# Two chunks of the hidden columns replaced by two passes over the rows, with the intermediate y kept in DRAM

## The chip, the cores and the metric

The kernel runs on one core of one Trainium2 chip. Its engines work at the same time, each through its own list of instructions: PE (TensorE) multiplies, DVE (VectorE) and ACT (ScalarE) add, scale and move results, POOL (GpSimd) and SP (SyncE) are used here mainly to start DMA transfers. The metric is device time of one execution in microseconds; several executions give a median. A separate profiled execution gives the span from its first to its last instruction and all rows below.

## The reference

The program computes two matrix products with a bias and a relu between them:

```python
x: (16, 512, 768)   w1: (768, 3072)   b1: (3072,)   w2: (3072, 768)     # all fp32
y = np.maximum(np.matmul(x, w1) + b1, 0)
return np.matmul(y, w2).astype(np.float32)
```

x has 8192 rows in all. The kernel holds operands as fp16 and sums in fp32 PSUM banks.

## The kernel before

**Products by sums.** Neither product is computed block by block in the plain way. Both use a bilinear scheme of the Strassen kind: sums and differences of blocks are made ahead of the multiplication, fewer products of such sums are formed, and the outputs are sums and differences of these products. Tables give each scheme: `X_SUMS` and `W1_SUMS` list the sums of operands, `FIRST_U` and `FIRST_V` say which two operands each product takes, `FIRST_OPS` says how a finished PSUM bank is evicted ("out" to the result, "sum" into an fp32 slot s, "seed" into the bank of another chain, with a bias where the table has one), and `FIRST_ORDER` is the order of the products. `Y_SUMS`, `W2_SUMS`, `SECOND_U`, `SECOND_V` and `SECOND_OPS` do the same for the second product.

**Chunks and blocks.** The 3072 hidden columns are cut into 2 chunks of 1536, the rows into 8 blocks of 1024. There are 16 iterations, 8 blocks of the first chunk and then 8 of the second (`plan` L1457, `iteration` L1479, `iteration_end` L1497). One iteration runs the first product of its block and chunk, then the second, and y never leaves SBUF.

First product (`add_first`): x as 4 row quarters of 256 by 2 halves of K, w1 as 2 halves of K by 3 thirds of the chunk, in 2 groups of 256 columns per third. A group takes 20 products where the plain form has 24. A product is 6 matmuls 128x256 (L1101). Evictions: ACT L1137 (512 wide) and L1141 (two halves of 256 with their own bias column), DVE L1144 (a custom instruction that adds a kept sum, applies the relu and writes y), L1147 and L1152. Iteration 0 runs its first product in the plain form (`first_block`, `plain` L998, evicted by ACT L1006), because no sum exists yet.

Second product (`add_second`): y as 4 by 4 blocks, w2 as 4 by 2, 26 products where the plain form has 32. A product is 6 matmuls 128x384 (L1229) into a pair of banks; evictions on ACT L1240 and DVE L1246. Sums of y are made on DVE (L1073, 28 per iteration, 8 of them in 4 fused instructions of 1536 columns), sums of x at L841 (16 per block), of w1 at L857 (12 per group and chunk), of w2 at L875 (18 per chunk). The first chunk's outputs are stored (L1279, SP, and L1281 and L1284), those of the second chunk are added to them in DRAM by accumulating DMAs of POOL (L1281, L1284); the last iteration loads the earlier outputs instead and adds them on chip (L1289).

**Loading.** x comes in by POOL DMAs that cast to fp16 (L717) and is transposed by SP DMAs (L772). The first block is transposed on PE instead (L938, with copies on DVE L946 and ACT L944): the first 512 rows come from SP and ACT queues as fp32, the second 512 by POOL as fp16. w1 strips come by POOL (L696), w2 by POOL (L702); the second chunk's weights are cast into DRAM in time and loaded by SP at iteration 8 (L1490, L1536). DVE makes tables of bias sums at the start (L973, L977) from b1, which PE turns (L958) and DVE copies (L962). ACT squares x, w1 and w2 (L780, L889, L903), sums of which must lie in a range at the end; otherwise `general_path` computes everything again.

**What sets the order.** All work is recorded as tasks with a cost, the tiles that it reads and writes, and a due time; a planner (`Graph.run`) then writes out one fixed order for each engine. An engine does not change its order later: an instruction that waits holds all behind it on that engine.

## Time and profile before

| | |
|---|---|
| time, median of 3 runs | 846.57 us (846.46 to 846.88) |
| span of the profiled execution | 845.1 us |
| profiled span against the median | 1.5 us less |
| PE busy | 838.5 us, 99% of the span |
| DVE busy | 735.7 us, 87% |
| ACT busy | 567.3 us, 67% |
| POOL busy | 172.5 us, 20% |
| DMA traffic | 128.93 MB, mean 153 GB/s |

Busy shares are means over stages that differ. A group row of the profile gives line, engine, operation, tiles and shape, then the number of instructions, busy time and mean duration in ns, then idle time ahead of them with what ended it. Where instructions of one engine overlap, busy time over count is less than the mean duration. The chain of work is a list of pieces: start, length, what ran.

### The profile page before, as it was taken

What the parts mean: (1) busy time and instruction counts of PE and PEld (TensorE: products, weight loads), DVE (VectorE), ACT (ScalarE), POOL (GpSimd) and SP (SyncE); (2) the same over time, 40 slices, a digit from 0 to 9 for tenths busy, and PEclk for the clock granted to TensorE, in tenths of its full rate; (3) what the DMA queues carried; (4) which work ended last, traced back from release to release, by engine and by line L of the source; (5) the groups of instructions that cost most, each with busy time, mean ns of one, the idle gap of its engine ahead of it and who ended that gap; (6) DMA issues with size and microseconds to landing.
All of it is one profiled execution on the core that took longest, in us unless ns stands there. A gap on an engine that the chain in (4) does not pass through costs nothing.

```text
span 845.1 us, 16822 instructions
## 1 busy us (share of the span) xinstructions
PE 838.5 (99%) x6383; PEld 625.4 (74%) x6383; DVE 735.7 (87%) x1229; ACT 567.3 (67%) x1199; POOL 172.5 (20%) x186
## 2 busy tenths in 40 slices
PE   9999999999999999999999999999999999999997
PEld 7668778686786867768687686877868678686874
DVE  5899988969789697988999979798896979979787
ACT  4866876779677684856858568766757666456462
POOL 6210011102011010110031503324041240501303
PEclk9999999999999999999999999999999999999999
DMA  9997498978988678593893977979789797986926
GB/s 210 205 180 189 84 221 115 166 180 132 215 113 162 158 133 190 104 226 136 238 176 67 190 127 123 186 106 178 127 128 147 118 172 113 143 138 76 177 86 169
DMA packets 171127, 128.93 MB, mean 153 GB/s; under 512 B 93964, under 2 KB 169508, under 8 KB 171044
## 3 DMA queue, kind: packets, MB, share of 16 engines
q0 software_dynamic: 56592, 68.82, 53.2%
q1 hardware_dynamic: 113984, 58.02, 29.0%
q8 instruction: 50, 0.82, 0.4%
q10 hardware_dynamic: 468, 1.00, 0.3%
q14 instruction: 33, 0.27, 0.1%
HBM read 73.54 MB, written 69.21 MB: 169 GB/s over the span
## 4 chain that ended last, share of the span: by engine, by line
PE 99%; DMA 1%; ACT 0%; issue 0%; ACTq 0%
PE ps L1229 48%; PE ps L1101 47%; PE ps L998 4%; DMA s<-in_x_dram 1%; PE ps L938 1%; ACT s L1240 0%; PE ps L958 0%; PE ps L1427 0%; PE ps L1438 0%; ACTq L1240 0%
## 5 line engine op out<-in xcount | busy, mean ns | idle before, releaser
L1229 PE MATMUL ps<-v,y 128*128 128x384 f16 x2496 | 408.2, 326 | 0.0
L1101 PE MATMUL ps<-x,v 128*128 128x256 f16 x3600 | 395.6, 273 | 0.0
L1101 PEld LDWEIGHTS <-v 128*128 128x128 f16 x3600 | 352.2, 98 | 42.3
L1229 PEld LDWEIGHTS <-y 128*128 128x128 f16 x2496 | 244.2, 98 | 159.9
L1240 ACT ACTIVATE s<-ps 128x384 f32<-128x384 f32 (+1 forms) x245 | 153.1, 643 | 125.4 <-PE ps L1229 124.9
L1073 DVE TENSOR_TENSOR y<-y 128x768 f16<-128x768 f16 (+1 forms) x384 | 219.0, 617 | 2.5
L1144 DVE CUSTOM_DVE_ANT_0 y<-ps,s 128x512 f16<-128x512 f32 x240 | 155.9, 685 | 52.9 <-ACT s L1141 40.1
L1281 POOL DMA_DIRECT2D out_dram<-s x78 | 93.9, 1475 | 144.8 <-ACT s L1240 91.8
L1141 ACT ACTIVATE s<-ps,bt 128x256 f32<-128x256 f32 x180 | 75.1, 469 | 62.8 <-PE ps L1101 56.5
L841 DVE TENSOR_TENSOR x<-x 128x768 f16<-128x768 f16 (+1 forms) x210 | 113.4, 577 | 1.2
L1141 ACT ACTIVATE y<-ps,bt 128x256 f16<-128x256 f32 x180 | 69.4, 485 | 10.8 <-PE ps L1101 10.8
L1240 ACT ACTIVATE ps<-ps 128x384 f32<-128x384 f32 (+1 forms) x143 | 67.0, 507 | 6.5 <-PE ps L1229 3.2
L1246 DVE TENSOR_TENSOR s<-ps,s 128x768 f32<-128x768 f32 x74 | 70.5, 952 | 0.9
L717 POOL DMA_DIRECT2D xn<-in_x_dram x30 | 25.9, 863 | 213.3 <-DMA x<-xn 101.0
L1246 DVE TENSOR_TENSOR s<-s,ps 128x768 f32<-128x768 f32 x60 | 57.0, 950 | 2.1
L780 ACT ACTIVATE junk<-xn 128x768 f16<-128x768 f16 x64 | 53.9, 843 | 0.3
L1284 POOL DMA_DIRECT2D out_dram<-s x15 | 17.8, 1184 | 168.6 <-ACT s L1240 156.9
L1141 ACT ACTIVATE ps<-ps,bt 128x256 f32<-128x256 f32 x60 | 26.7, 445 | 32.4 <-PE ps L1101 31.4
L1137 ACT ACTIVATE ps<-ps 128x512 f32<-128x512 f32 x60 | 35.3, 588 | 4.8 <-DVE y L1144 4.0
L1152 DVE TENSOR_TENSOR s<-s,ps 128x512 f32<-128x512 f32 x30 | 20.6, 687 | 17.8 <-PE ps L1101 17.8
L998 PE MATMUL ps<-x,v 128*128 128x256 f16 (+1 forms) x216 | 31.8, 308 | 0.0
L1147 DVE SCALAR_TENSOR_TENSOR s<-ps,bt,s 128x256 f32<-128x256 f32 x60 | 26.1, 476 | 4.4 <-PE ps L1101 4.4
(61 smaller groups left out, 310.0 us busy)
## 6 DMA issues: line engine op xcount, KB each, us to landing
out_dram<-s POOLq DMA_DIRECT2D x93, 384.0 KB, 8.6
out_dram<-s SPq DMA_DIRECT2D x69, 384.0 KB, 7.0
xn<-in_x_dram POOLq DMA_DIRECT2D x28, 768.0 KB, 9.6
v<-in_w_dram POOLq DMA_DIRECT2D x16, 192.0 KB, 7.6
x<-out_dram SPq DMA_DIRECT2D x14, 192.0 KB, 2.4
w1d<-in_w_dram POOLq DMA_DIRECT2D x6, 384.0 KB, 6.6
w2d<-in_w_dram POOLq DMA_DIRECT2D x12, 192.0 KB, 5.0
v<-w1d SPq DMA_DIRECT2D x12, 192.0 KB, 4.8
```

Of the source, the lines that this page charges most:

```text
L780: self.nc.scalar.activation(out=self.junk, in_=self.xn[:, s, :], func=ACTF.Square, accum_out=self.stat[:, self.stat_at["x"] + i:][:, 0:1])
L841: self.nc.vector.tensor_tensor(out=self.two(x, out), in0=self.two(x, in0), in1=self.two(x, in1), op=ALU.add if sign > 0 else ALU.subtract)
L998: nc.tensor.matmul(self.ps[:, ps.at[0], cols], lhsT=self.v1[:, gi, 2 * h + k2, k, j * P:(j + 1) * P], rhs=rhs, start=(first and k2 == 0 an ...
L1073: self.nc.vector.tensor_tensor(out=self.two(self.y, out), in0=self.two(self.y, in0), in1=self.two(self.y, in1), op=ALU.add if sign > 0 els ...
L1101: nc.tensor.matmul(self.ps[:, at, j * self.QM:(j + 1) * self.QM], lhsT=self.v1[:, gi, self.w1s[c][gi][FIRST_V[p]], k, j * P:(j + 1) * P], ...
L1137: nc.scalar.activation(out=out, in_=ps, scale=float(a), func=func if kind == "out" else ACTF.Copy)
L1141: nc.scalar.activation(out=out[:, j], in_=ps[:, j], func=func, scale=float(a), bias=beta(j))
L1144: nc.vector._custom_dve(TENSOR_ADD_SAT, out=out, in0=ps, in1=s, s0=F_MAX, s1=0.0)
L1229: nc.tensor.matmul(self.ps[:, bank[ch].at[j], 0:NH], lhsT=self.y[:, ys[SECOND_U[p]], m0:m0 + P], rhs=self.v2[:, slot[SECOND_V[p]], h, :], ...
L1240: nc.scalar.activation(out=out, in_=ps, func=ACTF.Copy, scale=float(a))
L1246: engine.tensor_tensor(out=out, in0=in0, in1=in1, op=ALU.add if a == b else ALU.subtract)
L1281: nc.gpsimd.dma_start(out=rows, in_=out, accum_op=ALU.add)
```

## The change

The two chunks go; in their place stand two passes over all rows.

- **Pass 1** forms the first product for all 8 blocks with all 3072 columns. x stays 4 by 2 blocks, w1 becomes 2 by 4, in 3 groups of 256 columns; a group takes 26 products where the plain form has 32 (L1077, 6 matmuls 128x256 each). The 39 rows of `FIRST_OPS` per group are 20 on ACT (13 with bias, as two halves of 256 each, L1105; 7 of 512, L1100) and 19 on DVE (10 custom instructions, L1111, and 9 plain ones, L1114, all 512 wide). Groups 0 and 1 of block 0 are plain (`PLAIN = 2`, L979), so 22 group passes use the scheme. Sums: 19 of x per block (L775), 18 of w1 per group (L787). The bias tables take 13 and 6 instructions (L946, L950) in place of 8 and 4.
- **y goes to DRAM**: results are written to 9 slots `yo` and stored by SP (384 stores of 128 KB, L961).
- **w2**: POOL casts it into DRAM during pass 1 (24 DMAs, L682). In the last block SP loads it into slots of v that w1 has left (24 loads), and DVE makes 18 sums for each of 3 groups, 54 in all (L847). They then stay for the whole of pass 2.
- **Pass 2** runs 16 half blocks of 512 rows (128 of each quarter). y comes back by SP (256 loads of 192 KB, L1174), DVE makes 28 sums per half block, none fused (L1191), and a product is 6 matmuls 128x384 over K quarters of 768 (L1228). Evictions are 384 wide, ACT L1244 and DVE L1248. Outputs are stored once by SP (L1258); accumulating POOL DMAs are left for half block 0 alone (`APART = (0,)`).
- **Checks** of the range re-read x, w1 and the cast w2 in pass 2 by 56 POOL DMAs (L873), squared by ACT (L877).
- x slots, y slots and their sums share one pool z of 46 slots. `EARLY` goes from 5 to 4: the second 512 rows of x are loaded and turned after 4 strips of w1 in place of 5.

PE's instructions go from 3600 to 3432 scheme matmuls 128x256, stay at 2496 of 128x384, and go from 144 of 256 and 72 of 512 to 144 of 256 and 120 of 512 in the plain form.

The diff, cut to its core:

```diff
-X_SUMS = ((23, 4, 6, -1), (22, 6, 7, -1), (9, 6, 5, -1), (11, 2, 5, -1), (14, 3, 5, -1), (19, 4,
...
+X_SUMS = ((8, 7, 6, 1), (9, 5, 7, -1), (10, 3, 2, 1), (11, 9, 6, -1), (12, 8, 1, -1), (13, 7, 1,
...
+FIRST_ORDER = (25, 19, 16, 3, 17, 6, 23, 21, 18, 15, 12, 8, 0, 20, 10, 2, 5, 14, 9, 11, 7, 4, 22, 1,
+    13, 24)
...
+EARLY, AHEAD = 4, 8
+
+POOL_X = ()
+FUSE_V2 = (((0,),), ((1,),), ((2,),))
+APART = (0,)
+
+Y_FUSE = ()
+
+NV, NZ, S_SLOTS, YO_SLOTS = 24, 46, 8, 9
+
+X_AT, X_GAP, STAGES, STAGE_AT, CHECKS = 0, 2, 4, 30, 3
+PLAIN = 2
...
-    NCH, QM, NG = 2, 256, 2
+    QM, NG = 256, 3
...
+        self.w1s = place({k * 4 + h: 2 * h + k for k in range(2) for h in range(4)}, W1_SUMS,
+                         FIRST_V, range(8, NV))
+        last = {FIRST_V[p]: i for i, p in enumerate(FIRST_ORDER)}
+        freed = [self.w1s[v] for v in sorted(last, key=lambda v: last[v])]
+        freed = [a for a in range(NV) if a not in freed] + freed
+        self.w2s = place(dict(enumerate(freed[:8])), W2_SUMS, SECOND_V, freed[8:])
+        self.free = list(range(16, NZ - SCRATCH))
+        self.scratch = {("", a): a for a in range(NZ - SCRATCH, NZ)}
+        self.touched, self.tick = dict.fromkeys(self.scratch.values(), 0), 0
...
-        self.v1 = one.tile([P, self.NG, 16, 3, 2 * P], FP16, name="v1")
-        self.v2 = one.tile([P, 24, 3, self.NH], FP16, name="v2")
-        self.y = one.tile([P, Y_SLOTS, 3 * self.QM], FP16, name="y")
-        self.x = one.tile([P, 20, 3, self.QM], FP16, name="x")
-        self.xn = one.tile([P, 8, self.K], FP16, name="xn")
-        self.s = one.tile([P, S_SLOTS, self.N], FP32, name="s")
+        self.v = one.tile([P, self.NG, NV, 768], FP16, name="v")
+        self.z = one.tile([P, NZ, 768], FP16, name="z")
+        self.s = one.tile([P, S_SLOTS, 512], FP32, name="s")
+        self.yo = one.tile([P, YO_SLOTS, 512], FP16, name="yo")
...
+        self.ydram = dram.tile([P, 2 * self.NB, 16, 768], FP16, name="yd")
+        self.w2dram = dram.tile([P, self.NG, 8 + len(W2_SUMS), 768], FP16, name="w2d")
...
+    def add_stage_w2(self, g, q, h):
+        h0 = (6 * q + 2 * g + h) * P
+        self.g.add("POOL", 850, lambda: self.nc.gpsimd.dma_start(
+            out=self.w2dram[:, g, q:q + 5:4, h * self.NH:(h + 1) * self.NH],
+            in_=self.w2[h0:h0 + P, :].rearrange("p (a n) -> p a n", a=2)), lat=15.0, dma=1.6,
+            writes=[("w2d", g, q, h)], after=[self.g.last_pe])
...
+    def add_w2_part(self, g):
+        slot = self.w2s
...
+        loads = [v for v in (*range(8), *early) if v in need]
+        for i in sorted(loads, key=lambda v: first[v] if v < 8 else 50 + first[v]):
+            self.load_w2(g, i, [("v", g, slot[i])], lambda i=i: self.v[:, g, slot[i]])
+            if i in W2_NEG:
+                self.g.add("ACT", 840, lambda a=slot[i]: self.nc.scalar.activation(
+                    out=self.v[:, g, a], in_=self.v[:, g, a], func=ACTF.Copy, scale=-1.0),
+                    writes=[("v", g, slot[i])])
+        for groups in FUSE_V2[g]:
+            for o, i, j, sign in left:
+                def add(a=slot[o], b=slot[i], d=slot[j], sign=sign, n=groups):
+                    n = slice(n[0], n[-1] + 1) if len(n) > 1 else n[0]
+                    self.nc.vector.tensor_tensor(
+                        out=self.v[:, n, a], in0=self.v[:, n, b], in1=self.v[:, n, d],
+                        op=ALU.add if sign > 0 else ALU.subtract)
+                self.g.add("DVE", 151 + 400 * len(groups), add, port=True,
+                           reads=[("v", n, slot[q]) for n in groups for q in (i, j)],
+                           writes=[("v", n, slot[o]) for n in groups])
...
+    def add_store_y(self, b, r, h, g, reg, n=0):
+        slot = 4 * r + h
+        t = self.g.add("SP", 100, lambda: self.nc.sync.dma_start(
+            out=self.ydram[:, 2 * b:2 * b + 2, slot, g * 256:(g + 1) * 256],
+            in_=self.yo[:, reg.at[n]].rearrange("p (s m) -> p s m", s=2)), lat=4.0, dma=0.42,
+            reads=[reg], writes=[("yd", b, slot, g)])
...
+        if PLAIN > 1:
+            self.rowed = [self.free.pop() for _ in range(8)][::-1]
+            outs = {}
+            for n in range(16):
+                if n % 2 == 0:
+                    self.add_load_x(1, n // 2)
+                run(self.plain(n % 8 // 2, n % 2, n // 8, outs, g=1))
...
         def product(p, ch, start):
             at = bank[ch].at[0]
-            gi, p = divmod(p, np)
+            a, w = xs[FIRST_U[p]], self.w1s[FIRST_V[p]]
             for j in range(2):
                 for k in range(3):
+                    x = self.z[:, a, k * self.QM:(k + 1) * self.QM]
                     nc.tensor.matmul(
-                        self.ps[:, at, j * self.QM:(j + 1) * self.QM],
-                        lhsT=self.v1[:, gi, self.w1s[c][gi][FIRST_V[p]], k, j * P:(j + 1) * P],
-                        rhs=self.x[:, self.xs[FIRST_U[p]], k, :],
+                        pairs(self.ps[:, at, :])[:, :, j],
+                        lhsT=self.v[:, g, w, k * self.QM + j * P:k * self.QM + (j + 1) * P],
+                        rhs=x.rearrange("p (s m) -> p s m", s=2),
...
+                        nc.scalar.activation(out=pairs(out)[:, :, j], in_=pairs(ps)[:, :, j],
+                                             func=func, scale=float(a),
+                                             bias=self.bt[:, n, g, j:j + 1])
...
+    def between(self, b, g, n):
+
+        for at in [x for x in self.later if x[:2] == (g, n)]:
+            self.later.remove(at)
+            at[2](*at[3])
+        if b + 1 < self.NB:
+            if b + 1 in self.xs:
+                self.next_x_sums(b + 1)
+        else:
+            self.next_y_loads(0)
+            self.next_y_sums(0)
...
+    def next_y_loads(self, t):
+
+        if t == 2 * self.NB:
+            return
+        slot = self.ys.setdefault(t, {})
+        while len(slot) < 16 and self.free:
+            i = Y_LOADS[len(slot)]
+            a = slot[i] = self.free.pop(0)
+            self.g.add("SP", 100, lambda i=i, a=a: self.nc.sync.dma_start(
+                out=self.z[:, a], in_=self.ydram[:, t, i]), lat=4.0, dma=0.6,
+                reads=[("yd", t // 2, i, g) for g in range(3)], writes=self.x_keys(a))
...
+        def product(p, ch, start):
+            for h in range(6):
+                nc.tensor.matmul(self.ps[:, bank[ch].at[0], 0:NH],
+                                 lhsT=self.z[:, ys[SECOND_U[p]], h * P:(h + 1) * P],
+                                 rhs=self.v[:, h // 2, slot[SECOND_V[p]],
+                                            h % 2 * NH:(h % 2 + 1) * NH],
+                                 start=(start and h == 0), stop=(h == 5), skip_group_check=True)
...
+            apart = what == "out" and u is not None and t in APART
+            if apart:
+                uses.remove(u)
+                self.g.add("SP", 100, lambda to=to, u=u: store(to, kept[u]), reads=[kept[u]],
+                           writes=[("out", t, to)], lat=3.5, dma=0.6)
+                dest = Reg("s")
+                self.g.add("ACT", 496, lambda n=n, dest=dest: operation(n, dest, alone=True),
+                           reads=reads, writes=[dest])
+                self.g.add("POOL", 900, lambda to=to, dest=dest: store(to, dest, e="POOL"),
+                           reads=[dest], writes=[("out", t, to)], lat=9.0, dma=1.3)
+                continue
...
+            for gi in range(0 if b else PLAIN, 3):
+                self.add_first(b, gi)
+                if gi == (X_AT if b else 1) and b + 1 < NB:
+                    self.add_x(b + 1)
+                if b + 1 == NB:
+                    self.add_w2_part(gi)
...
+        for t in range(2 * NB):
...
+            self.add_second(t)
+            for n in range(5 * t, min(5 * t + 5, 56)):
+                self.add_check_load(n)
```

**DVE at the start.** b1y is the turned bias, bt the tables of bias sums, v_65 (before) and v (after) w1 with its sums, z the pool of x. Before, from the copy of the bias to the copies of the second half of x:

```order
L962 COPY b1y<-ps 128x24
L973 TENSOR_SCALAR bt<-b1y 128x8 x2
L977 TENSOR_TENSOR bt<-bt,b1y 128x8
L973 TENSOR_SCALAR bt<-b1y 128x8 x3
L977 TENSOR_TENSOR bt<-bt,b1y 128x8
L973 TENSOR_SCALAR bt<-b1y 128x8
L977 TENSOR_TENSOR bt<-bt,b1y 128x8 x2
L973 TENSOR_SCALAR bt<-b1y 128x8 x2
L965 TENSOR_TENSOR stat<-b1y 128x24
L857 TENSOR_TENSOR v_65<-v_65 128x768 x12
L946 COPY x<-ps 128x3x128 x4
```

After, the same stretch:

```order
L775 TENSOR_TENSOR z<-z 128x768
L935 COPY b1y<-ps 128x24
L946 TENSOR_SCALAR bt<-b1y 128x6 x4
L950 TENSOR_TENSOR bt<-bt,b1y 128x6 x4
L946 TENSOR_SCALAR bt<-b1y 128x6
L950 TENSOR_TENSOR bt<-bt,b1y 128x6 x2
L946 TENSOR_SCALAR bt<-b1y 128x6 x8
L775 TENSOR_TENSOR z<-z 128x768 x3
L787 TENSOR_TENSOR v<-v 128x768 x7
L938 TENSOR_TENSOR stat<-b1y 128x24
L787 TENSOR_TENSOR v<-v 128x768 x6
L917 COPY z<-ps 128x3x128 x2
```

The copies of the second half of x (L946 before, L917 after) now stand behind 4 sums of x, 19 table instructions, the squared bias and 13 sums of w1, where they stood behind 12 table instructions, the squared bias and 12 sums of w1.

**DVE where the weights change.** Before, at the change from chunk 0 to chunk 1 (v_66 is w2, y the sums of y, s an fp32 sum, ps a PSUM bank), the sums of w2 (L875) stand among the evictions of a first product:

```order
L857 TENSOR_TENSOR v_65<-v_65 128x768 x14
L875 TENSOR_TENSOR v_66<-v_66 128x1152 x6
L1144 ISA y<-ps,s 128x2x256
L875 TENSOR_TENSOR v_66<-v_66 128x1152
L1144 ISA y<-ps,s 128x2x256
L1147 SCALAR_TENSOR_TENSOR s<-ps,bt,s 128x256 x2
L1144 ISA y<-ps,s 128x2x256 x2
L1152 TENSOR_TENSOR ps<-s,ps 128x512
L875 TENSOR_TENSOR v_66<-v_66 128x1152
L1147 SCALAR_TENSOR_TENSOR s<-ps,bt,s 128x256 x2
L1144 ISA y<-ps,s 128x2x256
L875 TENSOR_TENSOR v_66<-v_66 128x1152 x3
```

After, from the last eviction of pass 1 (L1111) on; L847 are sums of w2, L1191 sums of y, L1248 evictions of half block 0:

```order
L1111 ISA yo<-ps,s 128x512
L1191 TENSOR_TENSOR z<-z 128x768 x7
L847 TENSOR_TENSOR v<-v 128x768 x2
L1191 TENSOR_TENSOR z<-z 128x768 x4
L847 TENSOR_TENSOR v<-v 128x768
L1191 TENSOR_TENSOR z<-z 128x768 x2
L1248 TENSOR_TENSOR ps<-s,ps 128x384
L847 TENSOR_TENSOR v<-v 128x768 x3
L1248 TENSOR_TENSOR s<-ps,s 128x384
L847 TENSOR_TENSOR v<-v 128x768 x6
L1248 TENSOR_TENSOR s<-s,ps 128x384
L847 TENSOR_TENSOR v<-v 128x768 x9
```

Behind these rows stand one more eviction L1248, 3 sums L847, another L1248 and 12 sums L847. So 36 of the 54 sums of w2, 13 sums of y and 5 evictions follow the last eviction of pass 1. On PE, the 22nd product of half block 0 reads a sum of w2 that is followed by only 3 others.

1055 lines of the change are left out of this document (414 added, 641 removed), and 14 rows, old and new, of tables (FIRST_CHAINS, X_SUMS).

## Prediction

> **What bounds the kernel now.** I read the page first, for what is busy and whether TensorE runs at full clock:
>
> ```profile
> span 845.1 us, 16822 instructions
> PE 838.5 (99%) x6383; PEld 625.4 (74%) x6383; DVE 735.7 (87%) x1229; ACT 567.3 (67%) x1199; POOL 172.5 (20%) x186
> PEclk9999999999999999999999999999999999999999
> PE 99%; DMA 1%; ACT 0%; issue 0%; ACTq 0%
> ```
>
> PE is busy 99% of the span, its clock is granted in full in every slice, and the chain that ends last is PE itself. Next the chain in order of time, to see whether PE waits anywhere and what its pieces cost:
>
> ```profile
> 8.79 11.74 PE ps L998 x90
> 20.53 0.67 PE ps L938 x12
> 21.20 1.95 PE ps L998 x12
> ...
> 41.39 25.35 PE ps L1229 x156
> ...
> 118.35 26.20 PE ps L1101 x240
> ...
> 815.12 24.88 PE ps L1229 x153
> ```
>
> Each piece begins where the one before ends (20.53 + 0.67 = 21.20); from 5.66 us to 840 us PE never waits. So the pieces are prices of PE work with nothing else in them: 26.20/240 = 0.1092 us for a 128x256 matmul, 25.35/156 = 0.1625 for a 128x384, and 0.2163 for a 512-wide one (the piece of 1.95 us is 6 of 256 and 6 of 512: 1.95 - 6 x 0.1092 = 1.30, over 6). The wide ones read x in two runs and the price is still the work of two narrow ones, so the two-run reading that the change brings to the first product costs nothing here.
>
> PE without waits doesn't say how near the others are. The busy time by stretches does, for one second product and the first product behind it (busy us of PE, PEld, DVE, ACT, POOL):
>
> ```profile
> 93.00:118.30 25.30, 25.30 (x158) 15.27 (x157) 24.81 (x40) 18.77 (x39) 3.93 (x4) 1.00 0.82 152
> 118.30:144.50 26.20, 26.20 (x242) 23.48 (x240) 19.69 (x35) 19.88 (x45) 3.42 (x5) 1.00 0.71 148
> ```
>
> DVE is busy 98% of a second product and still late for nothing. So less PE work is time gained only if DVE keeps up in the new order.
>
> **The change part by part.** *PE's own work.* 168 scheme matmuls of 256 go (3600 to 3432): 168 x 0.1092 = 18.3 us less. 48 plain ones of 512 come: 48 x 0.2163 = 10.4 more. The second product keeps its 2496. Sum **-8.0 us**.
>
> *The loads of DVE and ACT in the steady stages.* The prices, from the groups kept apart by shape (count, then busy time and mean ns of one):
>
> ```profile
> L1073 DVE TENSOR_TENSOR y<-y 128x768 f16<-128x768 f16 x320 | 165.8, 550 | 2.0
> L1144 DVE CUSTOM_DVE_ANT_0 y<-ps,s 128x512 f16<-128x512 f32 x240 | 155.9, 685 | 52.9 <-ACT s L1141 40.1 <-PE ps L1101 9.2 <-DVE s L1147 0.2
> L841 DVE TENSOR_TENSOR x<-x 128x768 f16<-128x768 f16 x196 | 101.0, 551 | 1.2
> L1152 DVE TENSOR_TENSOR s<-s,ps 128x512 f32<-128x512 f32 x30 | 20.6, 687 | 17.8 <-PE ps L1101 17.8
> L1246 DVE TENSOR_TENSOR s<-ps,x 128x384 f32<-128x384 f32 x2 | 1.0, 546 | 0.0
> L1141 ACT ACTIVATE s<-ps,bt 128x256 f32<-128x256 f32 x180 | 75.1, 469 | 62.8 <-PE ps L1101 56.5 <-DVE s L1152 5.0 <-DMA out_dram<-s 0.5
> L1137 ACT ACTIVATE y<-ps 128x512 f16<-128x512 f32 x30 | 17.9, 597 | 15.9 <-PE ps L1101 15.8
> L1240 ACT ACTIVATE s<-ps 128x384 f32<-128x384 f32 x130 | 60.3, 496 | 22.9 <-PE ps L1229 22.4
> ```
>
> Busy time over count is less than the mean duration where one starts before the last has ended. A block of pass 1 is 3 groups of 26 products: PE 78 x 6 x 0.1092 = 51.1 us. DVE there: 30 custom evictions x 0.650 (155.9/240), 27 plain x 0.688, 19 x sums x 0.515 (101.0/196) = 47.9 us, 94%. ACT: 78 halves x 0.417 and 21 of 512 x 0.597 = 45.1 us, 88%. A half block of pass 2: PE 25.35, DVE 28 y sums x 0.518 and 12 evictions x 0.5 = 20.5 (81%), ACT 14 evictions x 0.46 = 6.4 and the squares of the checks in its idle time. Both stages are under PE, pass 1 narrowly (a rival below).
>
> *The start.* Here the order of DVE and the landing of x decide, so the rows are of DVE, then of POOL, then the page's transfer rate in 40 slices:
>
> ```profile
> 9.04 0.17 DVE L962 COPY b1y<-ps 128x24 f32<-128x24 f32 x1
> 9.25 0.31 DVE L973 TENSOR_SCALAR bt<-b1y 128x8 f32<-128x8 f32 x2
> 11.10 0.17 DVE L965 TENSOR_TENSOR stat<-b1y 128x24 f32<-128x24 f32 x1
> 20.81 0.62 DVE L946 COPY x<-ps 128x384 f16<-128x384 f16 x2 [0.66 <-PE ps L938]
> 24.16 5.27 DVE L857 TENSOR_TENSOR v<-v 128x768 f16<-128x768 f16 x10
> ```
>
> ```profile
> 20.59 0.71 POOL L702 DMA_DIRECT2D v<-in_w_dram  x1 [1.16 <-DMA xn<-in_x_dram]
> ```
>
> ```profile
> GB/s 210 205 180 189 84 221 115 166 180 132 215 113 162 158 133 190 104 226 136 238 176 67 190 127 123 186 106 178 127 128 147 118 172 113 143 138 76 177 86 169
> ```
>
> The second half of x lands at about 20.5, just as PE turns it (20.53). The change asks for it one strip sooner: PE saves 12 x 0.2163 = 2.6 us ahead of it and comes at 17.9. On the queue x is also one strip of 384 KB earlier, some 2 us at the 210 GB/s of the first slice, so it lands at about 18.5, and PE waits 0.6. Then PE has the turns (0.67) and a product of 1.3 and needs the copies at about 20.5. DVE has ahead of them, from 9.04: 4 x sums and 13 w1 sums at 5.27/10 = 0.527, 19 table instructions at (11.10 - 9.25)/12 = 0.154, 0.3 for copy and square: 9.0 + 9.0 + 2.9 + 0.3 = 21.2, and 0.62 for the copies, 21.8. That is 1.3 more. Sum **+1.9**; 0.8 with sums at 0.46 (next fence), 2.6 if x lands no sooner.
>
> *Between the passes.* 36 sums of w2, 13 of y and 5 evictions stand on DVE behind the last eviction of pass 1. Before, the like ran among evictions of a first product, which left DVE a quarter of its time. What such sums cost in a row is seen in DVE's timeline (start, length):
>
> ```profile
> 30.87 0.55 DVE L1073 TENSOR_TENSOR y<-y 128x768 f16<-128x768 f16 x1
> 31.34 0.55 DVE L857 TENSOR_TENSOR v<-v 128x768 f16<-128x768 f16 x1
> 31.80 0.75 DVE L875 TENSOR_TENSOR v<-v 128x1152 f16<-128x1152 f16 x1
> ```
>
> ```profile
> 401.28 1.28 DVE L1144 CUSTOM_DVE_ANT_0 y<-ps,s 128x512 f16<-128x512 f32 x2
> 402.48 7.14 DVE L1073 TENSOR_TENSOR y<-y 128x768 f16<-128x768 f16 x12
> ```
>
> A sum of 0.55 us lets the next begin after 0.47 (30.87 to 31.34), a custom eviction after 0.60 (two in 1.20). DVE comes out of pass 1 behind PE by an ACT eviction of 0.6 and three custom ones, some 2.6 us. The 22nd product of half block 0 needs the last sum of w2 but three: 13 + 33 = 46 sums and 5 evictions, 51 x 0.47 = 24.0, and 0.1 for the last to end: DVE is there at 26.7. PE gets there after 21 of 26 products, 21/26 x 25.35 = 20.5. So PE waits **+6.2 us**, in pieces, as each late sum comes; waits ahead of it are parts of the same lateness and do not add. At 0.52, as the run of w1 sums gives, it is 8.7; if the last evictions are ready when PE ends, 3.6. I take 0.47, since at 0.52 DVE in before's second products would also have been late, and wasn't. In the rest of pass 2 nothing of it is left: DVE has 25.35 - 20.5 = 4.9 us of room per half block.
>
> *Transfers.* The issues by line, with KB each and the median time to landing:
>
> ```profile
> out_dram<-s SPq DMA_DIRECT2D x69, 384.0 KB, 7.0
> x<-out_dram SPq DMA_DIRECT2D x14, 192.0 KB, 2.4
> v<-w1d SPq DMA_DIRECT2D x12, 192.0 KB, 4.8
> out_dram<-s SPq DMA_DIRECT2D x3, 192.0 KB, 2.6
> ```
>
> A store of y holds one of 9 slots; a block has 48 in 51.1 us, so a slot is wanted again after 9 x 1.06 = 9.6 us, and 192 KB lands in 2.4 to 4.8. A y load has the time of most of a half block ahead of its use. I charge **+0.6** for unseen waits of this kind: below it is 0, above 3; the nearest row is ACT's 0.5 us for a slot still being stored (L1141). The tail (last eviction and a 192 KB store, 2.6) is as before, within 0.5.
>
> *Sum*, against the profiled span: 845.1 - 8.0 + 1.9 + 6.2 + 0.6 = 845.8. The median of the runs lies 1.5 above that span, so **847.2 us**: no change.
>
> **The rivals.**
>
> *A, the forecast* (0.54): 847.2, by the bounds of its terms 844.5 to 850.
>
> *B, the changeover is hidden* (0.17): DVE is far enough ahead that no product waits for a sum of w2. For it: 98% busy without a wait in a second product. Against it: 51 instructions in 20.5 - 2.6 = 17.9 us would need 0.35 each, and no row has that. Price: 847.2 - 6.2 = 841.0, faster.
>
> *C, slower: DVE waits for ACT in pass 1* (0.16). DVE's custom evictions waited 40.1 us for ACT's sums, in 15 iterations of 2 groups 1.34 us per group. In before that hid in DVE's idle quarter; now a group has (51.1 - 47.9)/3 = 1.07 us of room. The excess, 0.27 x 22 groups = 6.0, would go to PE: 853.2. It decides as soon as DVE's waits pass 1.07 us per group. Against it: the order is new, and another order has other waits.
>
> *D, slower: sums that don't overlap* (0.07). If in a run of sums each starts when the last has ended, 51 cost 0.55 each, and PE waits 2.6 + 28.1 - 20.5 = 10.2; with 17 sums at the start, another 0.4: 851.6. The rows that start 0.47 apart speak against it, the run of ten at 0.527 partly for it.
>
> The Trainium skill, "VectorE: DVE Perf Modes", section "The DRAIN you can't avoid", says that the next Vector instruction does not start until the pipeline of the last is empty; by that rule the time is D's. Its section "Two Vector instructions with no wait between them" says that an instruction that isn't held starts earlier; by that one it is A's, and this trace agrees with it in its 0.47 for 0.55.
>
> *E, slower: y comes back late* (0.06). Each half block but the first starts late by what a load under traffic takes more than one alone, 4.8 - 2.4 = 2.4: 15 x 2.4 = 36, 883.
>
> That the change doesn't remove the products it says is excluded: they are counted in the order.
>
> **How the numbers follow.** 0.2%, 1.7 us, is about what a measurement of this kernel can tell from no change, so the same is 844.9 to 848.3. A lies there with half of its 0.54 (0.27), below with a fifth (0.11), above with the rest (0.16). Faster is 0.11 + 0.17 = 0.28, the same 0.27, slower 0.16 + 0.16 + 0.07 + 0.06 = 0.45. The range takes in B, C and D, since A alone or with one of them holds less than 8 in 10, and leaves out E: 840.5 to 853.5.
>
> **What would show it.** PE's busy time should fall by about 8 us, and its idle time should stand in two places: 0.8 to 2.6 us near 18 to 22 us, ahead of the products on the second half of x, released by the DMA of x and by DVE's copy; and 4 to 9 us in the first half block of pass 2, released by L847. In pass 1, PE's pieces should be 51.1 us per block without a gap; gaps released by L1111 or L1114 would be C. Gaps released by DMA of yd would be E. A changeover without waits (B), or starts of L847 rows 0.55 apart (D), would make the forecast wrong.

## The result, and the profile after

The changed kernel is slower: 910.50 us (median of 4 runs, 909.14 to 913.55) against 846.52 us (846.35 to 846.88) for the kernel before on the same chip, a ratio of 1.0759 (1.074 to 1.0779). The forecast was 847.2 us with a range of 840.5 to 853.5. The profiled execution took 909.62 us and has a span of 908.0 us, 62.9 more than before.

The page of the changed kernel, with the rows that answer to those of before:

```profile
span 908.0 us, 18203 instructions
...
PE 854.2 (94%) x6263; PEld 617.5 (68%) x6263; DVE 707.9 (78%) x1347; ACT 560.9 (62%) x1252; POOL 106.3 (12%) x174
...
PEclk9899999999999999989999999999999999999999
DMA  9998859869698696986878699999999999865411
```

PE now idles for 54 us, and its busy time rose by 15.7 us, although its instructions are fewer (the prediction's 8.0 us of work, from the same counts). Where it idles, PE's timeline shows; each row is a run of matmuls without a gap (gaps under some 0.15 us are merged), and the bracket is the idle time ahead of it with what ended it:

```profile
24.78 10.16 PE L979 MATMUL ps<-z,v 128*128 128x256 f16 x78
40.58 13.25 PE L979 MATMUL ps<-z,v 128*128 128x512 f16 x48 [5.63 <-ACT yo L989]
...
65.16 26.12 PE L1077 MATMUL ps<-z,v 128*128 128x256 f16 x234
...
392.54 3.00 PE L1077 MATMUL ps<-z,v 128*128 128x256 f16 x24 [0.65 <-DVE yo L1111]
398.89 49.77 PE L1077 MATMUL ps<-z,v 128*128 128x256 f16 x426 [3.35 <-DVE yo L1111]
...
486.08 9.19 PE L1228 MATMUL ps<-v,z 128*128 128x384 f16 x52
...
512.83 26.77 PE L1228 MATMUL ps<-v,z 128*128 128x384 f16 x162 [0.42 <-DVE v L847]
...
565.65 262.42 PE L1228 MATMUL ps<-v,z 128*128 128x384 f16 x1608 [2.12 <-ACT s L1244]
```

From these rows comes the bill of the 62.9 us, each part against the prices of the prediction (0.1092 us for a 128x256 matmul, 0.1625 for a 128x384):

| part | us | how worked out |
|---|---|---|
| PE's own work | -8.0 | as forecast, from the counts |
| block 0, plain form | +12.6 | ends at 65.16; without its stores (run e11 below) at 52.60 |
| scheme products of pass 1 | +46.1 | 486.08 - 65.16 = 420.9, less 3432 x 0.1092 = 374.8 |
| changeover to pass 2 | +6.3 | the 22nd product starts at 512.83, 26.75 after 486.08; 21 products are 126 x 0.1625 = 20.48 |
| just behind it | +5.0 | 512.83 to 565.65 is 52.8; its 294 matmuls are 47.8 |
| rest | +0.9 | |

Pass 1 has 58.7 us of it (12.6 and 46.1). The groups by shape say what PE waits for there, and what its releaser had waited for itself:

```profile
L1077 PE MATMUL ps<-z,v 128*128 128x256 f16 x3432 | 389.7, 276 | 31.4 <-DVE yo L1111 11.6 <-ACT s L1100 11.2 <-ACT ps L1105 2.5
L1111 DVE CUSTOM_DVE_ANT_0 yo<-ps,s 128x512 f16<-128x512 f32 x220 | 145.4, 684 | 54.4 <-DMA yd<-yo 38.5 <-PE ps L1077 13.2 <-ACT s L1100 1.5
L1100 ACT ACTIVATE yo<-ps 128x512 f16<-128x512 f32 x66 | 38.4, 595 | 12.4 <-DMA yd<-yo 8.7 <-PE ps L1077 1.7 <-issue 1.6
L979 PE MATMUL ps<-z,v 128*128 128x512 f16 x120 | 29.6, 406 | 6.7 <-ACT yo L989 6.6
L989 ACT ACTIVATE yo<-ps,b1y 128x512 f16<-128x512 f32 x32 | 21.2, 687 | 32.9 <-PE ps L979 17.7 <-DMA yd<-yo 15.2
```

PE's row names DVE and ACT. The rows of DVE and ACT name the DMA yd<-yo: an eviction can't write its slot of `yo`, because the store of what the slot held has not landed. All behind it on its engine stands, PSUM banks stay full, and PE stops. So gaps "released by L1111", which the prediction reserved for its rival C, are not C; one more step back in the trace tells them apart.

PE's gaps make up 31.4 of the 46.1 us. The other 14.9 are busy time, 389.7 in place of 374.8. About half of that is the clock: the granted clock is 0.98 in the mean from 65.16 to 486.08, and 2% of 389.7 is 7.8 us. Another part stands at full clock too: in run e3 below, with 1.00 over the same products, they are busy for 378.7 us, 3.9 more than the price. What is left, some 3 us, isn't apportioned. How the clock falls, stretches around the gap that ends at 398.89 show (start and end, length, busy us of PE, PEld, DVE, ACT, POOL, then granted clock, DMA share, GB/s):

```profile
394.00:396.00 2.00, 1.53 (x13) 1.15 (x12) 0.69 (x1) 1.69 (x5) 0.00 (x0) 1.00 0.88 204
396.00:398.00 2.00, 0.00 (x0) 0.00 (x0) 0.00 (x0) 0.63 (x2) 0.00 (x0) 0.93 1.21 78
398.00:400.00 2.00, 1.11 (x6) 0.78 (x6) 1.75 (x3) 0.53 (x1) 0.00 (x0) 0.50 0.81 194
400.00:402.00 2.00, 2.00 (x11) 1.38 (x10) 1.18 (x3) 0.89 (x3) 0.00 (x0) 0.50 0.88 207
402.00:404.00 2.00, 2.00 (x12) 1.36 (x10) 1.04 (x2) 0.94 (x2) 0.00 (x0) 0.50 0.90 248
404.00:406.00 2.00, 2.00 (x18) 1.69 (x17) 1.59 (x3) 0.69 (x3) 0.00 (x0) 0.87 0.50 138
```

A gap of 3.35 us is followed by some 5 us at half clock: from 398.89 to 404.00 PE starts 29 matmuls where 46 fit at 0.1092, so some 2 us are lost again.

What stands around the late stores is seen on SP's queue (start, length of the issuing, count) and on DVE in the same place, with the summary of all landings of the y stores behind them:

```profile
377.76 4.54 SPq L751 DMA_TRANSPOSE z<-z  x1
382.39 1.76 SPq L961 DMA_DIRECT2D yd<-yo  x2
384.24 3.22 SPq L751 DMA_TRANSPOSE z<-z  x2
...
393.85 1.05 SPq L961 DMA_DIRECT2D yd<-yo  x2
394.99 2.28 SPq L751 DMA_TRANSPOSE z<-z  x1
```

```profile
391.79 0.69 DVE L1111 CUSTOM_DVE_ANT_0 yo<-ps,s 128x512 f16<-128x512 f32 x1 [2.32 <-DMA yd<-yo]
398.14 1.29 DVE L1111 CUSTOM_DVE_ANT_0 yo<-ps,s 128x512 f16<-128x512 f32 x2 [3.29 <-DMA yd<-yo]
```

```profile
L961 SPq DMA_DIRECT2D yd<-yo x384: 359/439/2403, 12.9 to 491.0; - x192
...
DMA to landing us min/median/max: 1.8/2.1/13.1
```

In these stretches the DMA engines are full (share 0.81 to 1.21 in the rows up to 404). SP issues stores and transposes one behind the other, some of them at several times the usual length: over the run a store took up to 2.4 us where 0.44 is the median, and the first transpose of x for each of the blocks 3 to 7 took 3.55 to 4.54 us where 1.21 is the median. A store lands after up to 13.1 us where the median is 2.1; in block 0 alone (to 65 us) the median is 6.4. Nine slots bridge 9.6 us at the mean rate of a block, so they run out.

### The profile page after: what moved, and what is told of

Read it like the earlier page. It is cut to its first block, busy times and chain, and to the rows that moved or that the text cites. A ratio compares the mean times of both kernels' runs of the same rounds, so it can differ in the third digit from the quotient of the medians.

```text
span 908.0 us, 18203 instructions
## 1 busy us (share of the span) xinstructions
PE 854.2 (94%) x6263; PEld 617.5 (68%) x6263; DVE 707.9 (78%) x1347; ACT 560.9 (62%) x1252; POOL 106.3 (12%) x174
## 5 line engine op out<-in xcount | busy, mean ns | idle before, releaser
L1077 PE MATMUL ps<-z,v 128*128 128x256 f16 x3432 | 389.7, 276 | 31.4 <-DVE yo L1111 11.6
L1228 PE MATMUL ps<-v,z 128*128 128x384 f16 x2496 | 411.0, 326 | 7.3 <-ACT s L1244 3.5
L1077 PEld LDWEIGHTS <-v 128*128 128x128 f16 x3432 | 339.1, 99 | 82.0 <-issue 38.3
L1228 PEld LDWEIGHTS <-z 128*128 128x128 f16 x2496 | 243.7, 98 | 173.9 <-issue 12.0
L1191 DVE TENSOR_TENSOR z<-z 128x768 f16<-128x768 f16 x448 | 228.9, 551 | 21.9 <-DMA z<-yd 11.8
L1111 DVE CUSTOM_DVE_ANT_0 yo<-ps,s 128x512 f16<-128x512 f32 x220 | 145.4, 684 | 54.4 <-DMA yd<-yo 38.5
L1105 ACT ACTIVATE s<-ps,bt 128x256 f32<-128x256 f32 x352 | 146.7, 476 | 19.6 <-PE ps L1077 11.6
L1244 ACT ACTIVATE s<-ps 128x384 f32<-128x384 f32 x151 | 73.6, 487 | 109.5 <-PE ps L1228 97.8
L877 ACT ACTIVATE junk<-yo 128x768 f16<-128x768 f16 x112 | 93.8, 838 | 9.9 <-DMA yo<-in_x_dram 7.0
L1114 DVE TENSOR_TENSOR s<-ps,s 128x512 f32<-128x512 f32 x132 | 88.9, 683 | 6.0 <-PE ps L1077 4.5
L1248 DVE TENSOR_TENSOR s<-ps,s 128x384 f32<-128x384 f32 x107 | 59.4, 555 | 39.1 <-PE ps L1228 38.5
L1244 ACT ACTIVATE ps<-ps 128x384 f32<-128x384 f32 x80 | 37.8, 474 | 73.3 <-PE ps L1228 66.0
L775 DVE TENSOR_TENSOR z<-z 128x768 f16<-128x768 f16 x152 | 78.8, 550 | 4.3 <-PE ps L1077 2.4
L689 POOL DMA_DIRECT2D z<-in_x_dram x58 | 31.4, 543 | 297.4 <-PE ps L1077 274.2
L1100 ACT ACTIVATE s<-ps 128x512 f32<-128x512 f32 x66 | 39.7, 601 | 35.1 <-DVE ps L1114 20.6
L1105 ACT ACTIVATE yo<-ps,bt 128x256 f16<-128x256 f32 x132 | 54.8, 492 | 8.5 <-DVE s L1114 7.7
L1114 DVE TENSOR_TENSOR ps<-ps,s 128x512 f32<-128x512 f32 x66 | 45.1, 695 | 17.7 <-ACT s L1105 12.6
L979 PE MATMUL ps<-z,v 128*128 128x256 f16 (+1 forms) x264 | 45.5, 333 | 8.9 <-ACT yo L989 6.6
L1105 ACT ACTIVATE ps<-ps,bt 128x256 f32<-128x256 f32 x88 | 39.5, 449 | 22.2 <-PE ps L1077 18.7
L1248 DVE TENSOR_TENSOR s<-s,ps 128x384 f32<-128x384 f32 x62 | 34.2, 552 | 21.7 <-PE ps L1228 21.4
L1100 ACT ACTIVATE yo<-ps 128x512 f16<-128x512 f32 x66 | 38.4, 595 | 12.4 <-DMA yd<-yo 8.7
L979 PEld LDWEIGHTS <-v 128*128 128x128 f16 x264 | 26.4, 100 | 26.9 <-issue 13.0
```

Of the source, the lines that this page charges most:

```text
L775: (self.nc.gpsimd if e == "POOL" else self.nc.vector).tensor_tensor(out=self.z[:, a], in0=self.z[:, c], in1=self.z[:, d], op=ALU.add if si ...
L877: self.nc.scalar.activation(out=self.junk, in_=src, func=ACTF.Square, accum_out=None if at is None else self.stat[:, at:at + 1])
L979: nc.tensor.matmul(self.ps[:, ps.at[0], cols], lhsT=self.v[:, g, 2 * h + k2, k * self.QM + j * P:k * self.QM + (j + 1) * P], rhs=rhs, star ...
L1077: nc.tensor.matmul(pairs(self.ps[:, at, :])[:, :, j], lhsT=self.v[:, g, w, k * self.QM + j * P:k * self.QM + (j + 1) * P], rhs=x.rearrange ...
L1100: nc.scalar.activation(out=out, in_=ps, scale=float(a), func=func if kind == "out" else ACTF.Copy)
L1105: nc.scalar.activation(out=pairs(out)[:, :, j], in_=pairs(ps)[:, :, j], func=func, scale=float(a), bias=self.bt[:, n, g, j:j + 1])
```

## The experiments

Theory after this reading: the y stores share the DMA engines with the loads of x (POOL, casting), their transposes and, in block 0, the loads of w1; when all come together, stores land late and the 9 slots run out. Rivals: SP's list holds the stores behind transposes, in whatever state the DMA engines are (the expectations call this Q); the slots are too few; and the prediction's C, DVE waiting for ACT. The table gathers all runs, each against the kernel before on its own chip; the last column is the time from the first scheme product of pass 1 to the first product of pass 2 in the run's profiled execution, 374.8 of PE work. Where an edit adds lines, the line numbers behind it are shifted in that run's rows.

| run | median us | ratio (interval) | scheme products, us |
|---|---|---|---|
| the change | 910.50 | 1.0759 (1.074 to 1.0779) | 420.9 |
| e1 | 932.91 | 1.1017 (1.0971 to 1.1063) | 429.6 |
| e2 | 904.27 | 1.0679 (1.0647 to 1.071) | 407.7 |
| e3 | 874.11 | 1.0323 (1.0263 to 1.0382) | 383.7 |
| e4 | 909.86 | 1.0745 (1.0714 to 1.0776) | 416.2 |
| e5 | 899.35 | 1.0619 (1.0556 to 1.0682) | 405.2 |
| e6 | 900.67 | 1.0635 (1.0604 to 1.0666) | 388.8 |
| e7 | 900.87 | 1.0637 (1.0594 to 1.068) | 407.8 |
| e8 | 975.15 | 1.1514 (1.1465 to 1.1563) | 455.4 |
| e9 | 945.37 | 1.1166 (1.1108 to 1.1224) | 452.4 |
| e10 | 946.73 | 1.1182 (1.1119 to 1.1245) | 450.2 |
| e11 | 895.47 | 1.0577 (1.053 to 1.0624) | 414.0 |
| e12 | 902.37 | 1.0656 (1.0587 to 1.0724) | 407.3 |
| e13 | 912.27 | 1.0773 (1.0686 to 1.0859) | 415.3 |
| e14 | 959.88 | 1.1335 (1.1272 to 1.1398) | 426.2 |

**e1: the stores on POOL's queue.**

```diff
-        t = self.g.add("SP", 100, lambda: self.nc.sync.dma_start(
+        t = self.g.add("POOL", 550, lambda: self.nc.gpsimd.dma_start(
             out=self.ydram[:, 2 * b:2 * b + 2, slot, g * 256:(g + 1) * 256],
...
```

> The 384 stores of y are issued by POOL in place of SP; bytes, pieces and all else stay. Theory Q (SP's in-order list holds the y slots: a store is issued behind transposes that take 1.2 to 4.5 us each and may themselves wait for PE): most of the 58 us lost in pass 1 comes back, 855 to 875 us, and DVE's wait of 38.5 us for the stores falls under 10. Theory B (the DMA engines are full, the stores land late from whatever queue): 900 to 915, the wait stays. Theory C (DVE waits for ACT's sums and has too little room): within 10 us of 910.

Missed. With the stores off SP's list DVE waits as long for them as before (40.7 us after 38.5). They now stand behind the loads of x and w1 in POOL's list instead; at the start PE waits 18.0 us for that. So it is no clean test of SP's list, and shows only that POOL is no way out.

**e2: a higher planned cost of a store** (the planner then leaves more of SP's time around each).

```diff
-        t = self.g.add("SP", 100, lambda: self.nc.sync.dma_start(
+        t = self.g.add("SP", 520, lambda: self.nc.sync.dma_start(
```

> The planner is told that issuing a store costs SP 0.52 us, as the trace shows, not 0.10; it then spreads the transposes more among the stores, on the same queue. Theory Q: part comes back, 870 to 895. Theories B and C: within 10 us of 910.

A small gain, less than theory Q expected, and by the total (904.27) in the range of B and C. Pass 1 is 13.2 us shorter: DVE's waits for yd<-yo halve (19.3 us), and one gap of 2.2 to 2.9 us per block stays. SP's order has a part in it, not the whole.

**e3: only block 0's y is stored** (pass 2 reads that block's y each time).

```diff
+        if b:
+            return
         t = self.g.add("SP", 100, lambda: self.nc.sync.dma_start(
...
```

> Leaves out the stores of y of blocks 1 to 7; pass 2 reads block 0's y each time, so the output is wrong, with the same loads, products and sums. Theories Q and B: pass 1 loses almost nothing after block 0, 855 to 865 (the 11 us lost in block 0 stay). Theory C: DVE and ACT still wait for each other, 890 or more.

This settles the main point. PE's row of e3 from the middle of block 1 into block 7:

```profile
111.84 298.20 PE L1079 MATMUL ps<-z,v 128*128 128x256 f16 x2700 [0.63 <-DVE ps L1116]
```

2700 matmuls run without a gap (PE is busy for 297.24 of the 298.20 us). Without the stores pass 1 takes 37.2 us less, and all evictions, ACT's sums among them, are still there: C is refuted. The total, 874.11, lies between the two expectations: of the 46.1 us, 8.9 stay in the scheme products (block 0's third group is still stored), and pass 2 takes 422.4 in place of 418.3.

**e4: 11 slots in place of 9** (and 7 fp32 slots s in place of 8, for the room).

```diff
-NV, NZ, S_SLOTS, YO_SLOTS = 24, 46, 8, 9
+NV, NZ, S_SLOTS, YO_SLOTS = 24, 46, 7, 11
```

> 11 slots for y in place of 9, paid for with one slot of sums (7 in place of 8). Theories Q and B: a late store is waited for less, 885 to 903. Theory C: no gain, 908 or more, since the sums have less room.

No gain that the intervals can tell, which is what the expectation gave to C; e3 speaks against C. In the profiled executions pass 1 is 4.7 us shorter and pass 2 4.4 longer. DVE's waits for yd<-yo fall from 38.5 to 8.9 us, while those of ACT's L1100 rise from 8.7 to 17.3. Two slots more bridge 2 us, where landings are late by up to 11; and with a slot of sums fewer it is no clean test of the ring's length.

**e5: the loads of x apart**, 6 products from each other in place of 2 in the planner's time, and the transposes one group later.

```diff
-X_AT, X_GAP, STAGES, STAGE_AT, CHECKS = 0, 2, 4, 30, 3
+X_AT, X_GAP, STAGES, STAGE_AT, CHECKS = 1, 6, 4, 30, 3
...
-                self.later = [(0 if b else PLAIN, X_GAP * s, self.add_load_x, (b + 1, s))
+                self.later = [(*divmod(X_GAP * s, 26), self.add_load_x, (b + 1, s))
```

> The 8 loads of the next block's x stand 6 products (3.9 us) apart in place of 2, and its transposes follow them through the block; bytes and queues are the same. Theory D (the loads of x come in a burst that fills the DMA engines, and the stores of y that fall into it are late): the waits of 2 to 6 us per block in pass 1 go, 870 to 885 us. Theory S (the transposes in front of the stores in SP's list): the transposes stay, 900 or more.

The lowest median of the versions that leave nothing out, and still 6% over the kernel before. The loads did not come apart on the chip: six of a block's eight are issued between 243.88 and 247.72 and the other two by 249.54, since their place in the planner's time is an order on POOL's list and not a wait. In the changed kernel a block's eight are issued between 252.03 and 257.18; in both they begin some 5 us ahead of the block's first product. So the loads are neither spread nor later. What did change is SP's list: that block's eight transposes stand over 31 us (257.44 to 288.56), where the changed kernel has them over 20 (265.77 to 286.08). e5 therefore tests the transposes' places among the stores, as e2 does, and not the loads.

**e6: no loads of x for blocks 2 to 7** (those blocks read what the slots of z hold).

```diff
+        if b > 1:
+            return
         self.g.add("POOL", 760, lambda: self.load_x(b, s, a), lat=8.0, dma=1.05,
```

> Leaves out the loads of x of blocks 2 to 7 (the transposes turn old rows, the output is wrong); stores and transposes stay as they are. Theory D: pass 1 from block 2 on nearly without waits, 872 to 885. Theory S: 900 or more.

By the total, 900.67, this is theory S; but the total hides the answer: block 0 got worse in this order (its plain form ends at 83.69 in place of 65.16, on the same waits). From there on, with every store in place, e6's row is

```profile
114.10 319.81 PE L1079 MATMUL ps<-z,v 128*128 128x256 f16 x2892 [0.22 <-DVE ps L1116]
```

again without a gap. From 150 to 305 us of it a store lands after 4.1 us at most; from 154 to 324 of the changed kernel, after up to 12.6. So the stores are harmless without the loads, as the loads are without the stores: it takes both. Four stretches of about three blocks, of the kernel before, the changed kernel, e3 and e6 (columns as above), give DMA share and traffic for it:

```profile
93.00:247.00 154.00, 154.00 (x1184) 115.70 (x1183) 133.01 (x219) 115.72 (x251) 21.33 (x27) 1.00 0.84 160
```

```profile
154.00:324.00 170.00, 159.04 (x1404) 138.78 (x1404) 135.02 (x228) 125.25 (x298) 21.09 (x36) 0.98 0.87 181
```

```profile
150.00:303.00 153.00, 152.65 (x1391) 135.84 (x1390) 133.49 (x226) 123.77 (x294) 21.02 (x36) 1.00 0.52 75
```

```profile
150.00:305.00 155.00, 154.31 (x1405) 137.13 (x1403) 134.72 (x229) 124.09 (x297) 0.00 (x0) 1.00 0.64 153
```

The DMA engines were as busy before (0.84) as after (0.87), and PE did not wait. What is new is not the load but that a short ring of slots depends on one stream of it. At 0.52 and 0.64 there was room for that, at 0.87 there wasn't. The mean share alone doesn't rank the runs, though: over three blocks e7 (below) still has its gaps at 0.71, and e5 at 0.91 has 9.0 us of PE's idle time where the changed kernel at 0.87 has 11.0.

**e7: no transposes for blocks 3 to 7.**

```diff
-        for s in range(8):
+        for s in range(8 if b < 3 else 0):
             self.add_turn(b, s)
```

> Leaves out the transposes of x of blocks 3 to 7 (older x is used, the output is wrong); loads and stores stay. Theory S: 872 to 885. Theory D: the loads still collide with the stores, 895 or more. If e6 and e7 both land in the middle, it is the sum of loads, transposes and stores that fills the engines.

The total, 900.87, is in the range of D. Pass 1 takes 13.1 us less; DVE's waits for yd<-yo fall from 38.5 to 16.3 us, and gaps of 1.3 to 3.0 us stay in the later blocks, where SP has nothing but stores. So the transposes, by their place in the list (Q) or by their traffic, carry some 13 of the 46 us.

**e8: 18 of the 54 sums of w2 left out** (those of one group; the loads for the checks are also planned with more time to land).

```diff
-            for o, i, j, sign in left:
+            for o, i, j, sign in left if g < 2 else ():
...
-        self.g.add("POOL", 760, load, lat=13.0, dma=2.1 if n < nx + nw else 1.2,
+        self.g.add("POOL", 760, load, lat=20.0, dma=2.1 if n < nx + nw else 1.2,
```

> For pass 2 alone. Leaves out the 18 sums of w2 of the last group (stale weights, the output is wrong), and tells the planner that a check load lands after 20 us in place of 13. If DVE's run of sums behind pass 1 is what PE waits for in half block 0, its 6 us shrink to under 1 us (18 x 0.47 = 8.5 less on DVE). If the checks that ACT starts before their data is there hold its evictions, the 5 us of waits for ACT in half blocks 1 and 2 go too. Together 898 to 902 against 910; if neither is the cause, 908 or more.

For the changeover a hit, and the whole a miss. PE's rows at the changeover and later in pass 2:

```profile
520.02 60.79 PE L1228 MATMUL ps<-v,z 128*128 128x384 f16 x372
...
759.15 26.23 PE L1228 MATMUL ps<-v,z 128*128 128x384 f16 x150 [14.59 <-ACT s L1244]
```

With no sum of w2 behind pass 1, pass 2 starts without a wait: the 6.3 us are DVE's run of sums. But not 18 of them left that place, all did: the planner put the other 36 into the last block of pass 1 (450.6 to 495.4), which has gaps of 7.38 and 5.79 us, and pass 1 takes 34.5 us more. So the wait moved, and what fewer sums alone are worth isn't shown. In pass 2 runs of ACT's squares stand ahead of evictions (gaps of up to 14.59 us); which of the two edits did that wasn't tried.

**e9, e10 and e13: the loads of x held back.** A small POOL instruction ahead of each load reads a slot of `yo`, so that the load waits for an eviction. All three build on e5. In e9 the planner knows of it, e10 is e9 with e2's cost, and in e13 it is issued inside the load and the planner's order stays e5's.

```diff
+        if self.marked is not None:
+            self.g.add("POOL", 100, lambda r=self.marked: self.nc.gpsimd.tensor_copy(
+                out=self.good[0:1], in_=self.yo[0:1, r.at[0], 0:1]),
+                reads=[self.marked], writes=["mark"])
         self.g.add("POOL", 760, lambda: self.load_x(b, s, a), lat=8.0, dma=1.05,
...
```

> e5 once more, with something that really holds each load: ahead of it POOL reads one element of a y slot that the product at its place has just filled. (In e5 the 8 loads were still issued within 6 us, since nothing on the chip held them.) Theory D: the loads now stand some 4 us apart, the engines' share stays under 1.1, and the waits of pass 1 from block 1 on shrink from 46 us to 15 or less: 865 to 885. Theory S: 895 or more.

> e9 together with e2's cost of a store in the planner. Theory D: 1 to 8 us less than e9, by the stores' better places. Theory S: no less than e9.

Both missed, for a reason of their own: the planner gathered the sums of x, and DVE runs 9 of them (4.55 us from 208.11) ahead of an eviction, so PE waits 5.91 to 6.04 us in each of five blocks. They tell nothing of the loads.

```diff
+        def load():
+            if mark is not None:
+                self.nc.gpsimd.tensor_copy(out=self.good[0:1],
+                                           in_=self.yo[0:1, mark.at[0], 0:1])
+            self.load_x(b, s, a)
+        self.g.add("POOL", 760, load, lat=8.0, dma=1.05,
...
```

> e5's order unchanged on every engine but POOL, where each load of x first reads one element of the y slot filled last before its place (the planner doesn't know of it). It is e5 with loads that are really paced, without e9's long runs of x sums. If the burst is the cause, e5's waits of 2.0 to 2.3 us at the head of each block go: 875 to 888 against e5's 899. If the sum of the transfers is too much even when spread, 893 or more.

Here the loads do come apart (one block's start at 199.75, 201.40, 204.45, 210.03, 216.15, 219.68, 221.71 and 226.90), and the gaps stay. DVE's row at one of them:

```profile
236.19 0.69 DVE L1117 CUSTOM_DVE_ANT_0 yo<-ps,s 128x512 f16<-128x512 f32 x1 [3.26 <-DMA yd<-yo]
```

The burst of loads alone is not the cause either; spread, the same transfers kept the DMA engines full for longer (0.95 over three blocks, after e5's 0.91), and pass 1 takes 10.1 us more than e5's. Its stores land after 8.5 us at most, less than the 9.6 that the ring bridges at the mean rate, and DVE still waits 24.4 us for them. So the worst landing alone doesn't decide: a slot is also held while its store stands in SP's list (here behind a transpose of 3.21 us from 232.18); how evenly the results come wasn't measured.

**e11: block 0's y is not stored** (its half blocks read block 1's y).

```diff
+        if not b:
+            return
         t = self.g.add("SP", 100, lambda: self.nc.sync.dma_start(
...
```

> The reverse of e3: leaves out the stores of block 0 alone (pass 2 reads block 1's y for it, the output is wrong), where they compete with the loads of w1. If the stores are what PE waits for in block 0, its plain products end at 54 to 56 us in place of 65.2, and the whole at 895 to 900. If it is the start of x and DVE's tables, they end at 62 or later.

A hit (the plain form ends even earlier, at 52.60), and it shows the start by itself. PE's rows:

```profile
18.48 0.84 PE L909 MATMUL ps<-ident,z 128*128 128x128 f16 x12 [0.17 <-DMA z<-in_x_dram]
...
22.08 30.68 PE L981 MATMUL ps<-z,v 128*128 128x256 f16 x174
52.60 78.19 PE L1079 MATMUL ps<-z,v 128*128 128x256 f16 x702
```

The plain form runs without a gap but for 0.17 us for x. All of block 0's 12.6 us go with its stores.

**e12: wider pieces.** A store moves 128 pieces of 1024 B in place of 256 of 512 B; a y load moves 384 pieces of 512 B in place of 128 of 1536 B.

```diff
-        self.ydram = dram.tile([P, 2 * self.NB, 16, 768], FP16, name="yd")
+        self.ydram = dram.tile([P, self.NB, 16, 3, 2, 256], FP16, name="yd")
...
```

> y's layout in DRAM is turned: a store of 128 KB is now 128 pieces of 1024 bytes in place of 256 of 512, and a load of 192 KB is 384 pieces of 512 in place of 128 of 1536. If the number of pieces is what a transfer costs the DMA engines, pass 1 gets most of its 46 us back (its scheme products end by 460 in place of 486), and pass 2 becomes slower than 418 us by waits for y. If the bytes count, pass 1 ends within 8 us of 486 and pass 2 stays within 8 us of 418.

In between. Pass 1 gains 13.6 us, and DVE still waits 31.8 us for yd<-yo. Pass 2 takes 425.4 us after 418.3, but runs whose edit leaves pass 2 alone take 420.8 (e7) to 426.8 (e5), so nothing can be read from that. Wider stores are cheaper, and that is not enough. The Trainium skill, "DMA: Bandwidth & Descriptors", section "Specifications", puts the least transfer for line rate at 512 B, by which the stores of the change were wide enough; here 1024 B still took 13.6 us off pass 1.

**e14: the loads for the checks one half block later.**

```diff
-            for n in range(5 * t, min(5 * t + 5, 56)):
+            for n in range(max(0, 5 * t - 5), min(5 * t, 56)):
```

> Pass 2 alone: the check loads begin one half block later. If ACT's squares, which wait for late check loads, cost PE its 5 us in half blocks 1 and 2, the waits move one half block on and shrink to 3 or less: 906 to 909. If it is DVE's lateness after the changeover that costs them, nothing changes there: 910 within 1.5.

Missed: the planner gathered the squares elsewhere, and PE waits up to 7.23 us for ACT's evictions (L1244) later in pass 2; the changeover got worse too. What the 5.0 us behind the changeover are is therefore read, not tried. The chain of waits of the changed kernel passes there through the check loads and a square:

```profile
555.20 8.04 DMA yo<-in_x_dram
563.32 0.94 ACT junk L877 x2
564.31 0.72 issue
565.04 0.19 ACT junk L877
565.22 0.39 ACT s L1244
565.65 25.51 PE ps L1228 x156
```

A square (L877) waits for its load on ACT, and the eviction behind it waits with it. Two earlier gaps follow evictions that wait for a slot of s still being stored (2.03 and 1.90 us), so it isn't one cause alone.

## Why the prediction was wrong, point by point

**The step that failed** is the one on transfers: "A store of y holds one of 9 slots; a block has 48 in 51.1 us, so a slot is wanted again after 9 x 1.06 = 9.6 us, and 192 KB lands in 2.4 to 4.8", with 0.6 us charged, 3 at most. It measured 12.6 in block 0 (e11) and about 46 after it, of which 37 go with the stores (e3); beside no loads of x the same stores cost nothing (e6, from 114.10 to 433.91). The figures 2.4 and 4.8 were medians, and both of loads. The median landing of the y stores is 2.1 us, better than assumed; what holds the ring of slots up are the late ones, up to 13.1, and the time in SP's list ahead of them, in stretches in which the transfers of a block come together. The same table that gave 2.4 held 7.0 for the stores of before (384 KB), and before's DMA shares of 0.82 and 0.71 stood on the rows quoted for PE; neither was brought to bear on the slots. A second part of the cost, the clock (some 8 us), was not thought of: the PE row without a wait has only full clock to show.

**PE's own work**, -8.0: the counts are as forecast, and e3's and e6's pieces without gaps cost 0.1104 (298.20/2700) and 0.1106 (319.81/2892), 1% over the 0.1092, which is 4 us over the 3432. That the two-run reading costs nothing holds within this.

**The start**, +1.9: 0.68 us in the trace after for the landing of x, near the 0.6. The 1.3 for DVE's copies did not come. The copies start at 20.45 in place of 21.2, because the 19 small table instructions took 1.67 us (0.088 each) and not 19 x 0.154. PE's wait of 2.21 us there was on ACT's copies (L915), which stand behind an eviction that waited 4.11 for a y store.

**Between the passes**, +6.2: 6.3. Nine sums of the run begin 0.47 apart; DVE's row:

```profile
502.86 4.30 DVE L847 TENSOR_TENSOR v<-v 128x768 f16<-128x768 f16 x9
```

4.30 less the 0.08 by which a sum's 0.55 exceeds the spacing, over 9, is 0.47. Two small misses cancel in the total: DVE comes out of pass 1 3.3 us behind PE (its last eviction there begins at 488.79, the next instruction at 489.39), not 2.6, and PE's wait ends 23.4 after that, not 24.1. The forecast's price held, B is refuted (there is a wait) and D (0.55 apart) too. With it, of the two sections of the Trainium skill, "VectorE: DVE Perf Modes", that the prediction names, "Two Vector instructions with no wait between them", by which an instruction that isn't held starts earlier, is the one that this trace agrees with.

**The rivals C and E.** C needed DVE's waits for ACT to pass 1.07 us per group; they are 0.64 (12.6 of L1114 and 1.5 of L1111, over 22), and e3, with the same evictions, has no gap. E asked for y loads late in pass 2: behind the changeover PE has no gap released by a sum of y, and DVE's waits for z<-yd are 11.8 us in all. The gaps were to be "released by DMA of yd" for E; one step back they were, but by stores in pass 1, where the prediction had looked for loads in pass 2.

**A's bounds.** The plain sums of the bounds of its terms (start 0.8 to 2.6, changeover 3.6 to 8.7, transfers 0 to 3) are 842.9 to 852.8, not the 844.5 to 850 given for A; the result lies far above both.

**What stays open:** how the 46 us divide among bytes, piece sizes and transposes, since each of e2, e5, e7 and e12 takes 13 to 16 us and they were not put together; the causes of the 5.0 us behind the changeover; whether a longer ring alone would do (no run had more than 11 slots); and whether some other order could hide the stores. No version tried beats the kernel before.

## What to carry to other kernels

Where evictions write into a short ring of slots that a DMA empties, price the ring by the whole time that a slot is held in the busiest stretch (the wait in the issuing list and the late landings), not by the median landing, and ask first how full the DMA engines are there: here the streams of the kernel before ran at a share of 0.84 for free, and at 0.87 a stream that PSUM waits for did not. When PE's gaps are released by an eviction, follow the eviction one step further before naming its engine. Gaps on PE cost again in clock: here some 8 us for 31.4 us of gaps.
